# Fused four-layer encoder step: an early activation, weight parts split on two engines, the sample's tiles stacked for the transposes

## The chip, the core and the metric

The kernel runs on one core of a Trainium2 chip. The metric is device time in microseconds (us) for one execution. Five engines work side by side, each through its own instruction list in order: TensorE (PE, matrix products and transposes), VectorE (DVE), ScalarE (ACT), GpSimd (POOL) and SyncE (SP), which here issues every transfer (DMA). An instruction that waits holds back all that stands behind it on its own engine.

## The reference, cut to what matters

One inference step through four layers A, B, C, A. The input is 512 prompt tokens and 64 sample tokens, 1024 wide; the sample tokens attend to cached keys and values as well.

```python
for i in range(DEPTH):                      # kinds A, B, C, A
    z = rmsnorm(x, norm_g) @ w_in           # q, k, v and a gate in one projection
    q, k = rmsnorm(q, q_g), rmsnorm(k, k_g) # per head (C: low-rank q, latent kv, rotary part)
    o = attend(q, concat(cache, k), concat(cache, v), scale, bias, mask)
    x = x + (o * silu(gate)) @ w_out
return x_prompt, x_sample, new_a_k, new_a_v, new_b_k, new_b_v, new_c_kv, new_c_kr   # prompt and sample
```

A attends over a band of nine 64-token chunks with a relative bias, B over a window of 128 with four key heads and sinks, C over all the past through a 256-wide latent. The new keys and values and the rolled caches are outputs too.

## The kernel before

**Arithmetic.** Everything is 32-bit. Each operand of a product is split into a rounded high part and the rest, so one product is three matrix instructions. `load_w` (L132) loads a 128x512 weight piece (tile `ws`, L140 or L137), ACT writes its high part `wh` (L129) and the engine in `weng[0]` subtracts to get the low part `wl` (L130). That engine is POOL for the first eight pieces (`weng[0] = G` ahead of the opening loop) and DVE or POOL later. `wh` and `wl` have eight buffers each, `ws` four.

**Tiling.** The 576 tokens are four tiles of 128 and one of 64, the sample's. `mm_tok` (L161) is one tile's projection: three matrix instructions per piece for 128 tokens (L172 to L174). For the sample, its high and low parts are 128 columns of one operand, so there are two instructions (L177, L178), and the two halves of the result are added through the tile `hl` (ACT L182, DVE L183), which has one buffer.

**A unit** of work is one tile of one projection: `mm_tok`, a norm (`rstd`: DVE L124, POOL L125), a scaling into a tile of 128 x 512 (`qs`, three buffers; for the sample `half0` or `half1`, whose lower 64 rows stay zero), four or two PE transposes (`tr`, L187), and copies of the result out of PSUM.

**The opening.** For each of eight row blocks of the input, `x` and one weight piece are loaded, `feed` scales the block into `T` (ACT L199, DVE L200, ACT L202), squares it (ACT L204 for the first block, L207 then) and adds the squares (`acc`, DVE L208). `stats` then sums `acc` over partitions on PE (L213), from which the norms' factors `rr` come (DVE L215, POOL L217).

**Layer B** writes the newest keys to an output: for the last prompt tile and the sample tile DVE scales the transposed keys into a staging tile `st` (L529), and a DMA takes it to `bkT` (L530). `st`, like the cached keys' staging tile `kst`, is a buffer of the tag `hl`. **Layer C** loads the cached latent into a staging tile `cst`, also of tag `hl` (L790), issues six copies of caches from DRAM to DRAM behind it (`copy_caches`, L473 to L476), and splits `cst` into the high and low parts of the latent `lat` (ACT L129, POOL L130). POOL also makes the pow of each norm (L125) and the rotary parts of the queries (`qs`, L727 to L731). PE then transposes the queries and multiplies the latent with the key and value weights `kvb`.

**What sets the order.** Nothing is ordered by hand but the units of a stage. A scheduler with a timeline of its own decides when each instruction is put on its engine's list, so a small change can reorder lists far away from it. Buffers are rings: a tile with n buffers waits for the user n tiles ago.

Of the kernel before, what the change touches and what calls it, by code (L numbers as in the profile page):

```python
# [13 lines left out]
AF = mybir.ActivationFunctionType  # L14
# [14 lines left out]
QSB = 3  # L29
# [11 lines left out]
def encoder_step(ctx: ExitStack, tc: tile.TileContext, I, O):  # L41
# [12 lines left out]
    def sb(n, tag, bufs=None, dt=F32, pool=work):  # L54
        return pool.tile([128, n], dt, tag=tag, name=tag, bufs=bufs)
# [51 lines left out]
    ep = sb(5, "ep", pool=const)  # L107

# [77 lines left out]
    def tr(out, in_, perm=None):  # L186
        PE.transpose(out, in_, perm or ident)  # L187

# [116 lines left out]
    def layer_a(li, xT, first=None):  # L305
        w = I["a_w_in"][li]
        with tc.tile_pool(name=f"la{li}", bufs=1, reuse_waits="tile") as lp:
# [20 lines left out]
            def qk_units(pr):  # L328
                st = []

                def unit(t, t0, tn):
# [11 lines left out]
                    qs = rows_of(tn)  # L343
                    V.tensor_tensor(out=v3(qs[:tn], 128), in0=v3(p, 128), in1=bc(r.unsqueeze(2), tn, 4, 128), op=ALU.mult)
                    pt = v3(ps_t(), 128)
                    for j in range(4):
                        perm = ident if j > 1 else flip if tn == 128 else flip2
                        tr(pt[:, j, :], qs[:, j * 128 : j * 128 + 128], perm)
# [129 lines left out]
    def layer_b(xT):  # L478
        w = I["b_w_in"][0]
        with tc.tile_pool(name="lb", bufs=1, reuse_waits="tile") as lp:  # L480
# [14 lines left out]
            kst = v3(sb(512, "hl", 1), 128)  # L495
# [10 lines left out]
            for t, (t0, tn) in enumerate(TT):  # L506
# [18 lines left out]
                if t > 2:  # L525
                    o0 = t0 - 384
                    ld(O["bv"][o0 : o0 + tn], vt[:tn, t, :])
                    st = v3(sb(512, "hl", 1), 128)[:64, :, :tn]
# [5 lines left out]
            def q_units(g):  # L534
                w_ = []

                def unit(t, t0, tn):
# [10 lines left out]
                    qs = rows_of(tn)[:, :256]  # L548
                    V.tensor_tensor(out=v3(qs[:tn], 64), in0=v3(p, 64), in1=bc(r.unsqueeze(2), tn, 4, 64), op=ALU.mult)
                    pt = v3(ps_t()[:, :256], 128)  # L550
                    for j in range(2):
                        tr(pt[:, j, :], qs[:, j * 128 : j * 128 + 128])
# [138 lines left out]
    def layer_c(xT):  # L691
        w = I["c_w_in"][0]
        with tc.tile_pool(name="lc", bufs=1, reuse_waits="tile") as lp:
# [52 lines left out]
            for t, (t0, tn) in enumerate(TT):  # L746
# [5 lines left out]
                c = rows_of(tn)  # L752
                V.scalar_tensor_tensor(out=c[:tn], in0=p, scalar=r, in1=qag[:tn], op0=ALU.mult, op1=ALU.mult)
                pt = v3(ps_t(), 128)
                for j in range(4):
                    tr(pt[:, j, :], c[:, j * 128 : j * 128 + 128])
# [32 lines left out]
            cst = v3(sb(512, "hl", 1), 256)  # L789
# [167 lines left out]
    with tc.tile_pool(name="xp0", bufs=1) as xp:  # L957
        load_gain(0)
        for k in range(KD):
            xk = sb(TOK, f"x{k}", pool=xp)  # L960
            ld(xk, I["xT"][128 * k : 128 * k + 128, :])
            first.append(load_w([I["a_w_in"][0][128 * k : 128 * k + 128, 2048:2560]], 512))
            if k == 0:
                acc = new_acc(xp)
            feed(k, xk, gains[0], xT, xp, V, acc)
        ld(ident, I["ident"])
# [151 lines left out]
```

## Time and profile before

| | |
|---|---|
| median of three runs | 1255.45 us (1251.99 to 1255.57) |
| the profiled execution | 1254.89 us, of which the span of the trace is 1252.8 us |
| PE busy | 1225.8 us (98%) |
| DVE, ACT, POOL busy | 756.6 us (60%), 658.5 us (53%), 361.1 us (29%) |
| DMA | 125.11 MB, mean 100 GB/s |

The profile gives times from the start of the span. A row of a timeline is the start, the length, the engine, the line, the operation, the tile written and the tiles read, and in brackets how long the engine stood idle ahead of it and what ended that. PEclk is the clock granted to TensorE as a share of full speed. The rows of the changed kernel have other line numbers, 1 to 18 higher.

### The profile page before, as it was taken

Reading aid. Unit: us, or ns where it says so; the run is one execution under the profiler, and the core shown is the slowest. Engines: PE = TensorE matmul, PEld = TensorE weight load, DVE = VectorE, ACT = ScalarE, POOL = GpSimd, SP = SyncE. Lnnn points to the kernel's source line nnn. Section 1 sums busy time; section 2 is a strip of 40 time slices with the busy share of each in tenths; the row PEclk is TensorE's granted clock in tenths of the full one; section 3 lists DMA queues with packets and bytes.
Section 4 is the critical chain, followed back from the end, with each engine's and each line's share of the span. In section 5 each row is a group of like instructions: output and inputs, shape, how many; then the busy total and the mean of one; then the engine's idle time right before and its main releaser. Section 6 shows DMA issues by size and latency. Waiting matters only on the chain.

```text
span 1252.8 us, 22331 instructions
## 1 busy us (share of the span) xinstructions
PE 1225.8 (98%) x8015; PEld 1095.7 (87%) x8015; DVE 756.6 (60%) x2055; ACT 658.5 (53%) x1653; POOL 361.1 (29%) x425
## 2 busy tenths in 40 slices
PE   6999999999999999999999999999999999999998
PEld 5888898999989899899998887876998888889998
DVE  6266544755468888754577767676633665347552
ACT  5345543654436776643466767676533454436430
POOL 6422202222222120232285544440320322012130
PEclk9999999999999999999999999999999999999999
DMA  6333341434422231342272101112343233314331
GB/s 211 118 95 90 121 129 52 150 119 139 141 78 71 58 92 56 119 142 93 60 247 57 51 22 44 35 51 73 124 152 117 87 99 103 131 58 134 101 130 48
DMA packets 106046, 125.11 MB, mean 100 GB/s; under 512 B 11856, under 2 KB 83952, under 8 KB 105872
## 3 DMA queue, kind: packets, MB, share of 16 engines
q1 hardware_dynamic: 105936, 123.69, 31.7%
q8 instruction: 63, 1.03, 0.4%
q14 instruction: 47, 0.39, 0.1%
HBM read 103.73 MB, written 24.26 MB: 102 GB/s over the span
## 4 chain that ended last, share of the span: by engine, by line
PE 92%; DVE 3%; ACT 2%; issue 1%; DMA 1%; POOL 1%; SPq 0%; DVEq 0%; ACTq 0%
PE mm L174 11%; PE mm L173 11%; PE mm L172 11%; PE t L187 8%; PE mm L249 5%; PE mm L250 5%; PE mm L251 5%; PE mm L294 3%; PE mm L295 3%; PE mm L293 3%; PE o L412 3%; PE s L890 3%; PE mm L177 2%; PE mm L178 2%; PE o L900 2%; PE s L295 2%
## 5 line engine op out<-in xcount | busy, mean ns | idle before, releaser
L125 POOL TENSOR_TENSOR nv<-nv,mhalf 128x4 f32<-128x4 f32 (+6 forms) x127 | 139.8, 1108 | 350.1 <-DVE nv L124 306.7
L172 PE MATMUL mm<-wh,T 128*128 128x512 f32 (+2 forms) x600 | 217.5, 372 | 9.8 <-ACT wh L129 7.5
L173 PE MATMUL mm<-wl,T 128*128 128x512 f32 (+2 forms) x600 | 219.8, 369 | 0.0
L174 PE MATMUL mm<-wh,T 128*128 128x512 f32 (+2 forms) x600 | 219.5, 369 | 0.0
L130 DVE TENSOR_TENSOR wl<-ws,wh 128x512 fp32r<-128x512 f32 (+2 forms) x272 | 185.3, 696 | 47.4 <-ACT wh L129 43.3
L129 ACT ACTIVATE wh<-ws 128x512 fp32r<-128x512 f32 (+2 forms) x288 | 169.9, 615 | 65.8 <-PE mm L294 27.3
L249 PE MATMUL mm<-T,wh 128*128 128x288 f32 x512 | 155.7, 304 | 0.1
L250 PE MATMUL mm<-T,wh 128*128 128x288 f32 x512 | 153.5, 300 | 0.0
L251 PE MATMUL mm<-T,wl 128*128 128x288 f32 x512 | 153.3, 300 | 0.0
L172 PEld LDWEIGHTS mm<-wh,T 128*128 128x128 f32 x600 | 114.2, 191 | 26.4 <-ACT wh L129 7.5
L174 PEld LDWEIGHTS mm<-wh,T 128*128 128x128 f32 x600 | 114.6, 191 | 16.7 <-issue 0.2
L173 PEld LDWEIGHTS mm<-wl,T 128*128 128x128 f32 x600 | 114.9, 192 | 16.1 <-issue 0.5
L249 PEld LDWEIGHTS mm<-T,wh 128*128 128x128 f32 x512 | 96.2, 188 | 3.1 <-issue 1.9
L250 PEld LDWEIGHTS mm<-T,wh 128*128 128x128 f32 x512 | 96.3, 188 | 1.8 <-issue 1.7
L259 POOL TENSOR_TENSOR o<-o,sq 128x288 f32<-128x288 f32 x52 | 45.4, 874 | 179.7 <-DVE sq L257 91.3
L251 PEld LDWEIGHTS mm<-T,wl 128*128 128x128 f32 x512 | 96.1, 188 | 1.0 <-issue 1.0
L294 PE MATMUL mm<-oT,wh 128*128 128x288 f32 x320 | 94.7, 297 | 0.5 <-DVE oT L279 0.5
L293 PE MATMUL mm<-oT,wh 128*128 128x288 f32 x320 | 93.3, 297 | 1.9 <-ACT oT L278 1.9
L295 PE MATMUL mm<-oT,wl 128*128 128x288 f32 x320 | 94.0, 296 | 0.0
L382 DVE CUSTOM_DVE_ANT_0 ex<-s,bias 128x128 f32<-128x128 f32 (+1 forms) x64 | 30.4, 484 | 57.8 <-PE s L404 46.7
L293 PEld LDWEIGHTS mm<-oT,wh 128*128 128x128 f32 x320 | 59.9, 189 | 2.3 <-ACT oT L278 2.3
L294 PEld LDWEIGHTS mm<-oT,wh 128*128 128x128 f32 x320 | 60.4, 189 | 1.5 <-DVE oT L279 1.5
(289 smaller groups left out, 2886.4 us busy)
## 6 DMA issues: line engine op xcount, KB each, us to landing
ws<-in_a_w_in SPq DMA_DIRECT2D x64, 256.0 KB, 3.0
ws<-in_a_w_in SPq DMA_DIRECT2D x128, 128.0 KB, 2.3
ws<-in_b_w_in SPq DMA_DIRECT2D x40, 256.0 KB, 3.2
ws<-in_a_w_out SPq DMA_DIRECT2D x32, 256.0 KB, 3.1
xd<-x SPq DMA_DIRECT2D x24, 288.0 KB, 3.0
x<-xd SPq DMA_DIRECT2D x24, 288.0 KB, 5.9
ws<-in_c_w_in SPq DMA_DIRECT2D x24, 256.0 KB, 3.2
x<-in_xT SPq DMA_DIRECT2D x16, 288.0 KB, 6.3
```

The costliest lines, as they stand in the source:

```text
L125: G.tensor_tensor(out=r, in0=r, in1=bc(mhalf[:tn], tn, n), op=ALU.pow)
L129: S.activation(h, src, AF.Copy)
L130: (eng or G).tensor_tensor(out=l, in0=src, in1=h.bitcast(F32), op=ALU.subtract)
L172: PE.matmul(out, xh, h[:, ws], start=(i == 0), stop=False)
L173: PE.matmul(out, xh, l[:, ws], start=False, stop=False)
L174: PE.matmul(out, xl, h[:, ws], start=False, stop=(i == last))
L249: PE.matmul(p, wh, xT[:, k, cs], start=(k == 0), stop=False)
L250: PE.matmul(p, wh, xT[:, k, ls], start=False, stop=False)
L251: PE.matmul(p, wl, xT[:, k, cs], start=False, stop=(k == KD - 1))
L293: PE.matmul(p, wh, oT[:, k, cs], start=(k == 0), stop=False)
L294: PE.matmul(p, wh, oT[:, k, ls], start=False, stop=False)
L295: PE.matmul(p, wl, oT[:, k, cs], start=False, stop=(k == KD - 1))
```

## The change

1. At the very beginning ACT squares one column of a constant into one column of `rr`, which is written again later.
2. In the opening loop `weng[0]` alternates: DVE makes `wl` of the pieces 0, 2, 4 and 6, POOL of 1, 3, 5 and 7. Behind the loop it is POOL again.
3. `pairs_of` is new. Units of a 128-token tile are as before. For the sample, two 64-row blocks go one under the other into a full `qs` tile, by two DVE operations of half the width, and one transpose takes both: two in place of four in layers A and C, one in place of two in layer B. `half0` and `half1` stay in use elsewhere.
4. `kst` and `st` in layer B take a buffer of the tag `ex` (four of them), and `cst` in layer C one of `sq` (two), in place of `hl`.

PE's list is 22 transposes shorter.

```diff
@@ -105,6 +105,7 @@
     rb = sb(TOK, "rb", pool=const)
     rr = sb(5, "rr", pool=const)
     ep = sb(5, "ep", pool=const)
+    S.activation(rr[:, 0:1], mhalf, AF.Square)
 
     late = [None]
     weng = [V]
@@ -185,6 +186,16 @@
 
     def tr(out, in_, perm=None):
         PE.transpose(out, in_, perm or ident)
+
+    def pairs_of(tn, n, w, op):
+        qs = rows_of(tn) if tn == 128 else sb(512, "qs", QSB)
+        pt = v3(ps_t()[:, : n * tn], tn)
+        if tn == 128:
+            op(v3(qs[:, : n * w], w), slice(0, n))
+        else:
+            for e in range(2):
+                op(v3(qs[64 * e : 64 * e + 64, : n * w // 2], w), slice(e, n, 2))
+        return qs, pt, 128 // tn
 
     def hl_evac(dst_h, dst_l, src):
         S.activation(dst_h, src, AF.Copy)
@@ -340,12 +351,13 @@
                     ss = sb(4, "nss", pool=tiny)[:tn]
                     V.tensor_reduce(out=ss, in_=v3(sq, 128), axis=AX, op=ALU.add)
                     r = rstd(ss, tn, 4, 1.0 / 128, t)
-                    qs = rows_of(tn)
-                    V.tensor_tensor(out=v3(qs[:tn], 128), in0=v3(p, 128), in1=bc(r.unsqueeze(2), tn, 4, 128), op=ALU.mult)
-                    pt = v3(ps_t(), 128)
-                    for j in range(4):
-                        perm = ident if j > 1 else flip if tn == 128 else flip2
-                        tr(pt[:, j, :], qs[:, j * 128 : j * 128 + 128], perm)
+                    def put(out, js):
+                        V.tensor_tensor(out=out, in0=v3(p, 128)[:, js], in1=bc(r[:, js].unsqueeze(2), tn, out.shape[1], 128), op=ALU.mult)
+
+                    qs, pt, n = pairs_of(tn, 4, 128, put)
+                    for i in range(4 // n):
+                        perm = ident if i * n > 1 else flip if tn == 128 else flip2
+                        tr(pt[:, i * n : i * n + n, :], qs[:, i * 128 : i * 128 + 128], perm)
                     cs = slice(t0, t0 + tn)
                     V.tensor_scalar(out=kf[:, :, cs], in0=pt[:, 2:4, :tn], scalar1=kg, scalar2=None, op0=ALU.mult)
                     if t in (0, 4):
@@ -492,7 +504,7 @@
             vc = sb(256, "vc", pool=lp)
             ld(vc, I["cache_b_v"][0, 0].rearrange("t h d -> t (h d)"))
 
-            kst = v3(sb(512, "hl", 1), 128)
+            kst = v3(sb(512, "ex", 4), 128)
             with tc.issue_after(late[0]):
                 for e in range(2):
                     ld(kst[64 * e : 64 * e + 64], I["cache_bkT"].rearrange("h p t -> p h t"))
@@ -525,7 +537,7 @@
                 if t > 2:
                     o0 = t0 - 384
                     ld(O["bv"][o0 : o0 + tn], vt[:tn, t, :])
-                    st = v3(sb(512, "hl", 1), 128)[:64, :, :tn]
+                    st = v3(sb(512, "ex", 4), 128)[:64, :, :tn]
                     V.tensor_scalar(out=st, in0=pt[:64, :, :tn], scalar1=kg[:64], scalar2=None, op0=ALU.mult)
                     ld(O["bkT"].rearrange("h p t -> p h t")[:, :, o0 : o0 + tn], st)
 
@@ -545,11 +557,15 @@
                     ss = sb(4, "nss", pool=tiny)[:tn]
                     V.tensor_reduce(out=ss, in_=v3(sq, 64), axis=AX, op=ALU.add)
                     r = rstd(ss, tn, 4, 1.0 / 64, t)
-                    qs = rows_of(tn)[:, :256]
-                    V.tensor_tensor(out=v3(qs[:tn], 64), in0=v3(p, 64), in1=bc(r.unsqueeze(2), tn, 4, 64), op=ALU.mult)
-                    pt = v3(ps_t()[:, :256], 128)
-                    for j in range(2):
-                        tr(pt[:, j, :], qs[:, j * 128 : j * 128 + 128])
+                    def put(out, js):
+                        i0, n = (js.start, 2) if js.step else (0, 4)
+                        src, f = (p, r) if n == 4 else (p[:, 128 * i0 : 128 * i0 + 128], r[:, 2 * i0 : 2 * i0 + 2])
+                        V.tensor_tensor(out=out.rearrange("p a (b c) -> p (a b) c", c=64), in0=v3(src, 64),
+                                        in1=bc(f.unsqueeze(2), tn, n, 64), op=ALU.mult)
+
+                    qs, pt, n = pairs_of(tn, 2, 128, put)
+                    for i in range(2 // n):
+                        tr(pt[:, i * n : i * n + n, :], qs[:, i * 128 : i * 128 + 128])
                     for e in range(2):
                         a, b = slice(64 * e, 64 * e + 64), slice(64 - 64 * e, 128 - 64 * e)
                         dst = q[:, e, :, t0 : t0 + tn] if t < 4 else qm[:, :, e, :]
@@ -749,11 +765,13 @@
                 junk = sb(512, "sq", 2)[:tn]
                 S.activation(junk, p, AF.Square, accum_out=ss)
                 r = rstd(ss, tn, 1, 1.0 / 512, t)
-                c = rows_of(tn)
-                V.scalar_tensor_tensor(out=c[:tn], in0=p, scalar=r, in1=qag[:tn], op0=ALU.mult, op1=ALU.mult)
-                pt = v3(ps_t(), 128)
-                for j in range(4):
-                    tr(pt[:, j, :], c[:, j * 128 : j * 128 + 128])
+
+                def put(out, js):
+                    V.scalar_tensor_tensor(out=out, in0=v3(p, 128)[:, js], scalar=r, in1=v3(qag, 128)[:tn, js], op0=ALU.mult, op1=ALU.mult)
+
+                c, pt, n = pairs_of(tn, 4, 128, put)
+                for i in range(4 // n):
+                    tr(pt[:, i * n : i * n + n, :], c[:, i * 128 : i * 128 + 128])
                 l0 = lo_at(t0, TOK)
                 hl_evac(cq[:, :, t0 : t0 + tn], cq[:, :, l0 : l0 + tn], pt[:, :, :tn])
 
@@ -786,7 +804,7 @@
                 S.activation(ckv[:, :, k0 : k0 + tn], pt[:, 0:2, :tn], AF.Copy)
                 V.tensor_tensor(out=ckv[:, :, l0 : l0 + tn], in0=pt[:, 0:2, :tn],
                                 in1=ckv[:, :, k0 : k0 + tn].bitcast(F32), op=ALU.subtract)
-            cst = v3(sb(512, "hl", 1), 256)
+            cst = v3(sb(512, "sq", 2)[:, :512], 256)
             copy_caches(ld(cst, I["cache_ckvT"].rearrange("(k p) t -> p k t", p=128)))
             l0 = lo_at(SEQ, NK)
             split(ckv[:, :, 512:768], ckv[:, :, l0 : l0 + PAST], cst)
@@ -959,10 +977,12 @@
         for k in range(KD):
             xk = sb(TOK, f"x{k}", pool=xp)
             ld(xk, I["xT"][128 * k : 128 * k + 128, :])
+            weng[0] = (V, G)[k % 2]
             first.append(load_w([I["a_w_in"][0][128 * k : 128 * k + 128, 2048:2560]], 512))
             if k == 0:
                 acc = new_acc(xp)
             feed(k, xk, gains[0], xT, xp, V, acc)
+        weng[0] = G
         ld(ident, I["ident"])
         end = stats(xp, acc)
         ld(flip, I["flip"])
```

**DVE in the opening.** Before (`T` are the low parts of the blocks, `acc` the sums of squares):

```order
L200 SCALAR_TENSOR_TENSOR T_98<-x0_103,ga0_94,T_98 128x576
L200 SCALAR_TENSOR_TENSOR T_98<-x1_117,ga0_94,T_98 128x576
L208 TENSOR_TENSOR acc_111<-acc_111,xsq_128 128x576
L200 SCALAR_TENSOR_TENSOR T_98<-x2_131,ga0_94,T_98 128x576
L208 TENSOR_TENSOR acc_111<-acc_111,xsq_142 128x576
L200 SCALAR_TENSOR_TENSOR T_98<-x3_145,ga0_94,T_98 128x576
L208 TENSOR_TENSOR acc_111<-acc_111,xsq_156 128x576
L200 SCALAR_TENSOR_TENSOR T_98<-x4_159,ga0_94,T_98 128x576
L208 TENSOR_TENSOR acc_111<-acc_111,xsq_170 128x576
```

After:

```order
L211 SCALAR_TENSOR_TENSOR T_99<-x0_104,ga0_95,T_99 128x576
L131 TENSOR_TENSOR wl_109<-ws_106,wh_108 128x512
L211 SCALAR_TENSOR_TENSOR T_99<-x1_118,ga0_95,T_99 128x576
L219 TENSOR_TENSOR acc_112<-acc_112,xsq_129 128x576
L211 SCALAR_TENSOR_TENSOR T_99<-x2_132,ga0_95,T_99 128x576
L219 TENSOR_TENSOR acc_112<-acc_112,xsq_143 128x576
L131 TENSOR_TENSOR wl_137<-ws_134,wh_136 128x512
L211 SCALAR_TENSOR_TENSOR T_99<-x3_146,ga0_95,T_99 128x576
L219 TENSOR_TENSOR acc_112<-acc_112,xsq_157 128x576
L211 SCALAR_TENSOR_TENSOR T_99<-x4_160,ga0_95,T_99 128x576
L219 TENSOR_TENSOR acc_112<-acc_112,xsq_171 128x576
```

Two of the four `wl` that DVE has taken over (L131) stand among these rows; the other two follow behind the next blocks. On PE, 67 matrix instructions stand ahead of `stats` in both orders.

**PE in layer C,** where the queries are transposed. Before (`mm_7953` are keys and values from the latent `lat` and the weights `kvb`, `t` the transposed queries):

```order
L173 MATMUL mm_7953<-wl_7944,lat_7046 128x256
L174 MATMUL mm_7953<-wh_7943,lat_7046 128x256
L172 MATMUL mm_7953<-wh_7949,lat_7046 128x256
L173 MATMUL mm_7953<-wl_7950,lat_7046 128x256
L174 MATMUL mm_7953<-wh_7949,lat_7046 128x256
L187 MATMUL t_7698<-ident_76,qs_7679 96x128 x4
L187 MATMUL t_7737<-ident_76,qs_7718 96x128 x4
L187 MATMUL t_7776<-ident_76,qs_7757 96x128 x4
```

After (`mm_7917` is the gate's sum that stood ahead of `mm_7953`, now `mm_7958`; `t_7703` to `t_7781` are the queries):

```order
L261 MATMUL mm_7917<-T_6517,wh_7808 128x288
L262 MATMUL mm_7917<-T_6517,wl_7809 128x288
L188 MATMUL t_7703<-ident_76,qs_7684 96x128 x4
L188 MATMUL t_7742<-ident_76,qs_7723 96x128 x4
L188 MATMUL t_7781<-ident_76,qs_7762 96x128 x4
L173 MATMUL mm_7958<-wh_7948,lat_7051 128x256
L173 MATMUL mm_7987<-wh_7948,lat_7051 128x256
```

The twelve keys-and-values instructions that stood ahead of the three groups of transposes now stand behind them.

**POOL in layer C,** a little earlier. Before (`lat` is the latent's low part, `nv` the pows of three query tiles, `krz` and `qs` rotary parts):

```order
L731 TENSOR_TENSOR krz_7053<-r1_7589,r2_7590 64x32
L125 TENSOR_TENSOR nv_7686<-nv_7686,mhalf_81 128x8
L125 TENSOR_TENSOR nv_7725<-nv_7725,mhalf_81 128x8
L125 TENSOR_TENSOR nv_7764<-nv_7764,mhalf_81 128x8
L130 TENSOR_TENSOR lat_7046<-hl_7604,lat_7046 128x2x256
L817 TENSOR_TENSOR qs_7679<-qs_7679,nv_7686 128x4x32
```

After:

```order
L131 TENSOR_TENSOR lat_7051<-sq_7609,lat_7051 128x2x256
L747 TENSOR_TENSOR krz_7058<-r1_7594,r2_7595 64x32
L126 TENSOR_TENSOR nv_7691<-nv_7691,mhalf_81 128x8
L126 TENSOR_TENSOR nv_7730<-nv_7730,mhalf_81 128x8
L126 TENSOR_TENSOR nv_7769<-nv_7769,mhalf_81 128x8
L835 TENSOR_TENSOR qs_7684<-qs_7684,nv_7691 128x4x32
```

The split of the latent stood behind the three pows and now stands ahead of them. On SP the load of the latent and the six cache copies moved ahead of the loads of the two `kvb` pieces.

**PE at the end of layer B.** Before (`o_6145` are the prompt heads, `o_6215` the sample's attention, `mm_6460` the output projection):

```order
L627 MATMUL o_6145<-pb_6143,v_3668 64x256 x2
L627 MATMUL o_6145<-pb_6136,v_3668 64x256 x2
L627 MATMUL o_6145<-pb_6066,v_3668 64x256 x2
L627 MATMUL o_6145<-pb_6059,v_3668 64x256 x2
L666 MATMUL o_6215<-pts_6213,vc_3670 64x128 x2
L669 MATMUL o_6215<-pts_6213,v_3668 64x128 x2
L293 MATMUL mm_6460<-oT_6257,wh_6438 128x288
```

After (the same tiles are `o_6150` and `o_6220`):

```order
L261 MATMUL mm_6393<-T_3156,wh_6283 128x288
L262 MATMUL mm_6393<-T_3156,wl_6284 128x288
L260 MATMUL mm_6393<-T_3156,wh_6283 128x288
L261 MATMUL mm_6393<-T_3156,wh_6283 128x288
L262 MATMUL mm_6393<-T_3156,wl_6284 128x288
L260 MATMUL mm_6393<-T_3156,wh_6289 128x288
L261 MATMUL mm_6393<-T_3156,wh_6289 128x288
L262 MATMUL mm_6393<-T_3156,wl_6290 128x288
L260 MATMUL mm_6393<-T_3156,wh_6289 128x288
L261 MATMUL mm_6393<-T_3156,wh_6289 128x288
L262 MATMUL mm_6393<-T_3156,wl_6290 128x288
L682 MATMUL o_6220<-pts_6218,vc_3671 64x128 x2
```

Eleven gate instructions (L260 to L262) moved in between the prompt heads' products and the sample's.

## Rows read from the trace of the kernel before

**Rows 1.** The page: engines' busy time, the chain, one group of instructions.

```profile
PE 1225.8 (98%) x8015; PEld 1095.7 (87%) x8015; DVE 756.6 (60%) x2055; ACT 658.5 (53%) x1653; POOL 361.1 (29%) x425
...
PE 92%; DVE 3%; ACT 2%; issue 1%; DMA 1%; POOL 1%; SPq 0%; DVEq 0%; ACTq 0%
...
L130 DVE TENSOR_TENSOR wl<-ws,wh 128x512 fp32r<-128x512 f32 (+2 forms) x272 | 185.3, 696 | 47.4 <-ACT wh L129 43.3
```

**Rows 2.** Waits of PE: line, releaser: us in total, times, longest.

```profile
PE mm L172 <- DVE hl L183: 2.6, 2, 2.3
...
PE mm L293 <- ACT oT L278: 1.9, 2, 1.0
...
PE o L666 <- ACT o L303: 0.8, 1, 0.8
```

**Rows 3.** Timelines of ACT, PE, DVE and POOL in the opening.

```profile
4.25 1.28 ACT L199 ACT_TABLE_LOAD   x1 [4.25 <-DMA x<-in_xT]
...
7.47 1.65 PE L172 MATMUL mm<-wh,T 128*128 128x512 f32 x3 [7.47 <-ACT wh L129]
...
27.05 1.47 PE L213 MATMUL t<-ones,acc 128*128 128x2 f32 x10 [2.48 <-DVE acc L208]
...
9.32 0.75 DVE L208 TENSOR_TENSOR acc<-acc,xsq 128x576 f32<-128x576 f32 x1
...
11.75 1.85 DVE L208 TENSOR_TENSOR acc<-acc,xsq 128x576 f32<-128x576 f32 x1
...
23.41 3.58 DVE L208 TENSOR_TENSOR acc<-acc,xsq 128x576 f32<-128x576 f32 x2
...
7.49 1.28 POOL L130 TENSOR_TENSOR wl<-ws,wh 128x512 fp32r<-128x512 f32 x1 [5.20 <-ACT wh L129]
...
17.51 5.36 POOL L130 TENSOR_TENSOR wl<-ws,wh 128x512 fp32r<-128x512 f32 x3 [2.75 <-ACT wh L129]
```

**Rows 4.** Windows: busy us (instructions) of each engine, PEclk, DMA share, GB/s.

```profile
27.00:31.00 4.00, 3.95 (x16) 3.46 (x17) 0.66 (x7) 0.04 (x1) 2.21 (x3) 0.62 0.74 200
...
369.00:372.00 3.00, 3.00 (x17) 3.00 (x16) 2.42 (x9) 1.20 (x4) 2.06 (x3) 0.55 0.13 33
...
526.00:529.00 3.00, 1.23 (x13) 0.87 (x12) 1.00 (x3) 2.07 (x7) 1.59 (x2) 1.00 0.94 272
529.00:533.00 4.00, 3.99 (x19) 3.76 (x18) 3.99 (x4) 3.59 (x8) 3.80 (x3) 0.59 0.96 331
...
644.00:648.00 4.00, 2.79 (x20) 2.29 (x21) 0.15 (x1) 2.14 (x6) 3.56 (x10) 1.00 0.64 203
```

**Rows 5.** Timelines of DVE, ACT and PE in layer B, 361 to 372.

```profile
363.80 0.73 DVE L529 TENSOR_SCALAR hl<-t,par 64x512 f32<-64x512 f32 x1
...
367.38 0.59 ACT L182 ACTIVATE hl<-mm 64x512 f32<-64x512 f32 x1 [1.62 <-DMA out_bkT<-hl]
...
368.84 0.36 PE L172 MATMUL mm<-wh,T 128*128 128x256 f32 x1 [2.29 <-DVE hl L183]
```

**Rows 6.** Timeline of PE, layer B: four sample transposes and the next.

```profile
373.28 0.60 PE L187 MATMUL t<-ident,half 128*128 128x128 f32 x4
373.71 0.38 PE L187 MATMUL t<-ident,qs 128*128 128x128 f32 x2
```

**Rows 7.** Timelines of PE, POOL and ACT in layer C, 630 to 652.

```profile
644.21 0.39 PE L172 MATMUL mm<-wh,lat 128*128 128x256 f32 x1 [0.27 <-DVE hl L183]
...
645.75 1.27 PE L187 MATMUL t<-ident,qs 128*96 128x128 f32 x8
648.00 0.64 PE L187 MATMUL t<-ident,qs 128*96 128x128 f32 x4 [0.98 <-POOL qs L731]
...
634.28 4.95 POOL L125 TENSOR_TENSOR nv<-nv,mhalf 128x8 f32<-128x8 f32 x3
...
647.49 0.45 POOL L731 TENSOR_TENSOR qs<-r,r 128x128 f32<-128x128 f32 x1
...
636.18 0.63 ACT L129 ACTIVATE lat<-hl 128x512 fp32r<-128x512 f32 x1 [2.00 <-DMA hl<-in_cache_ckvT]
```

## The prediction

> **What bounds the kernel now.** I read the page first: PE is busy 98% of the span and makes up 92% of the chain that ended last [rows 1]. So time is won in three ways only: PE gets fewer instructions, it waits less, or it runs less at half clock. Then I read the list of PE's waits [rows 2]: they are few and short, so each has a place of its own. I went to those places that the change touches, in timelines of the engines there [rows 3, 5, 7], and last to windows that show the granted clock beside the busy time [rows 4], because a wait of PE can be paid twice.
>
> The second payment is in [rows 4]. After the wait of 2.48 us at 27.05 [rows 3] the window from 27 to 31 has a granted clock of 0.62 with PE fully busy; after the wait of 2.29 at 368.84 [rows 5] it is 0.55; after a stretch of 3.00 us with PE busy for 1.23 it is 0.59. That is a mix of the two levels, 2.4 and 1.2 GHz. The last of these windows gives the price: (1 − 0.59) × 4.00 = 1.6 us of work not done. A window with 1.21 us of idle PE in 4.00 (644 to 648) kept 1.00. So a short wait costs itself, and one over 2 us costs itself and 1.6 more.
>
> **The change part by part.**
>
> *The opening, start.* ACT's table load takes 1.28 us and starts only when the first block of x has landed, at 4.25 [rows 3]. PE's first matrix instruction waits on ACT's first `wh`, at 7.47. With the one-column activation ahead, which waits on no transfer, the load runs before 4.25, ACT's chain starts 1.28 earlier, and so does PE: 7.47 − 1.28 = 6.2. The added activation costs nothing as long as the transfer covers it. PE then runs the same 67 instructions up to the sums of `stats` without a wait, in both orders; it came there at 27.05 − 2.48 = 24.57 and now comes at 23.3.
>
> *The opening, end.* There PE waits for the last `acc` on DVE, which ends at 23.41 + 3.58 = 26.99 [rows 3]. DVE and POOL hinder each other: the same `acc` addition takes 0.75 alone and 1.85 beside a POOL subtraction, 1.10 more; POOL's takes 1.28 alone and 5.36 / 3 = 1.79 when they alternate. So the two engines' work adds up rather than overlaps. The Trainium skill has the reason (SBUF — State Buffer, Who interferes with whom): an operation of VectorE with two SBUF inputs and one of GpSimd that reads SBUF hold a shared port in turn, each for its whole length. That speaks against splitting the low parts over two engines; if the two ran side by side, the last `acc` would be done before PE arrives and the gain would be 0.7 larger than I take below. By the rows, four subtractions leave POOL, 4 × 1.28 = 5.1, and four come to DVE, at 0.70 each [rows 1], 2.8. The sum shrinks by 2.3. The earlier start is worth between 0.4 and 1.28 here, because the transfers of later blocks do not come earlier. The last `acc` ends between 26.99 − 3.6 = 23.4 and 24.3. I take 24.0 for PE's start, near the later end, since every x has to land at its old time: a gain of 27.05 − 24.0 = 3.05, and a wait of 0.7 in place of 2.48. Bounds: 1.28 (the wait stays as long) and 3.75 (none is left). A wait of 0.7 is nearer to the window that kept its clock than to the three that lost it, so 1.6 more are saved. Together 4.65.
>
> *Layer B, the wait for `hl`.* DVE writes the staging tile at 363.80 and a DMA reads it; only when that has landed may ACT write the one buffer again for the sample tile, at 367.38; DVE adds the halves, and PE waits 2.29 for it at 368.84 [rows 5]. With `st` in another ring the sample's halves are added as soon as PE has made them. The wait of 2.3 goes, with the half clock behind it: 3.9. What is late next is DVE, busy 2.42 of the 3.00 us from 369 to 372 [rows 4]. Bounds: 0 (DVE gives it all back) and 3.9. I take the upper, because with the wait gone DVE has the idle time of that stretch ahead as well.
>
> *Layer B, end.* PE waits 0.8 for the prompt heads' copies (L303) and then, in one of the two waits on `oT`, 1.0 [rows 2]. Eleven gate instructions now stand in the first of these; they are PE work that was there anyway, so 0.8 is saved. The second wait stays, its cover is gone with them. Whether the half clock of 529 to 533 [rows 4] goes too is open: 0 to 1.6. I take 0, because PE still does only eight short products between two waits.
>
> *Transposes.* 22 go. Four take 0.43 from start to the next start [rows 6], 0.108 each: 2.4. All but two stand among other PE work in layers A and B. The 13 added DVE operations, of half the width, lie beside that: DVE is at 60% of the span [rows 1]. Bounds: 0 (each falls into a wait) and 2.4.
>
> *Layer C.* Before, PE spent 644.21 to 645.75, that is 1.5 us, on twelve keys-and-values instructions while POOL made the rotary parts, and waited 0.98 for the last of these, which ended at 647.49 + 0.45 = 647.94 [rows 7]. Now the transposes come first, and PE stands from about 643.8 until the same 647.94, with only the transposes to do: the twelve instructions come behind and cost 1.5. Idle time is then over 2 of some 4 us, nearer to the window of 526 to 529 than to that of 644 to 648 [rows 4], so I count 1.6 for the clock. The loss is 3.1; its bounds are 0 (POOL is done sooner) and 5.6 (below, E).
>
> *The rest* of layers A, B and C is put in another order here and there with no wait on either side that the trace shows; I take 0, with 1.5 either way.
>
> **Sum.** 4.65 + 3.9 + 0.8 + 2.4 − 3.1 = 8.65. Against the profiled execution, 1254.89 (a span of 1252.8 and 2.1 around it), that is 1246.2; against the median of 1255.45, which is 0.56 higher, **1246.8**. The median is what will be compared, so this is the forecast.
>
> **The rivals.**
>
> A. *The clock does not follow the length of the wait.* For: between the long waits and the window that stayed at 1.00 the trace has few cases. Then half clock stays in the opening, or comes anew elsewhere: one to two times 1.6, so 1248.4 to 1250.0. The Trainium skill (TensorE: Matmul & The Clock Gate, What's actually happening) says that the window in which activity is judged runs freely and isn't set by the kernel's start; by that, where a wait falls decides with its length. No row here shows that phase.
>
> B. *The opening keeps its wait.* If the transfers and not the sum of DVE and POOL set the last `acc`, everything moves by the 1.28 of the start alone, the wait stays near 2.5 and the clock drops: 1246.8 + 4.65 − 1.28 = 1250.2. Against it: the last rows of DVE stand packed with POOL's [rows 3].
>
> C. *DVE takes the place of `hl`.* In layer B DVE is the next engine, and 3.9 come back as waits on it a little later: 1250.7.
>
> D. *It does little of what it says:* two of B, C and "the transposes fall into waits" at once. B and C give 1246.8 + 3.4 + 3.9 = 1254.1, B and the transposes 1246.8 + 3.4 + 2.4 = 1252.6.
>
> E. *Slower.* In layer C POOL's split of the latent now stands ahead of the three pows, which started at 634.28 before [rows 7]. POOL takes its list in order, so if the cached latent lands late, the pows, the rotary parts and PE's transposes wait for it, one for one. ACT had the latent at 636.18 and took 0.63 over it [rows 7]; at that time POOL would stand for 636.8 − 634.3 = 2.5 us: 1249.3. Slower than before it gets when the landing is 8.65 later than POOL's arrival, about 642.3 on the old scale, 6 us after the old landing; slower by over 0.3% from about 646. For it: six cache copies and the weights share the transfers there. Against it: the load now stands ahead of the copies, and needs no buffer of `hl`.
>
> **Chances.** Forecast 0.45, with a range of its own from 1243 to 1250; A 0.12; B 0.15; C 0.10; D 0.10; E 0.08. 0.3% is 3.8 us, about what a measurement of this kernel can tell from no change: under 1251.7 is faster, over 1259.2 slower. Faster is most of the forecast, A and B, and two thirds of C: 0.79. Same is D and the tails of B, C and E: 0.16. Slower is half of E and a little of the unseen: 0.05. The low end, 1242.5, has the clock kept in layer C (1.6) and at the end of layer B (1.6), and a little for no wait in the opening; the high end, 1253.5, reaches into D.
>
> **What would show it.** PE's first instruction at 6.2, `stats` on PE at 24.0 after a wait under 1, and a clock of 1.00 from 24 to 28. No wait on `hl` in layer B, and no window under 1.00 there. The sample's attention at the end of layer B without a wait in front. Around the queries' transposes in layer C, waits of PE on POOL's `qs` of together 3 us. 22 transposes fewer. Wrong would be: a wait of over 2 us on `acc`, a new wait on DVE in layer B over 2 us, or POOL standing for the latent.

## The result, and the profile after

The changed kernel takes 1245.16 us (median of four runs, 1244.52 to 1248.99) where the kernel before took 1255.18; the ratio is 0.9929, 95% interval 0.9917 to 0.9941, so 7.4 to 10.4 us less. 1246.8 was forecast. Two later series of the same kernel gave 0.9930 (0.9916 to 0.9944) and 0.9912 (0.9897 to 0.9926).

The page of the changed kernel: span, busy time of each engine.

```profile
span 1243.5 us, 22309 instructions
...
PE 1220.9 (98%) x7993; PEld 1090.6 (88%) x7993; DVE 757.0 (61%) x2072; ACT 659.6 (53%) x1654; POOL 353.4 (28%) x421
```

The share of PE is as before [rows 1]: it has 22 instructions fewer, and the span is 9.3 us shorter. The waits of PE (line, releaser: us in total, times, longest), to be read against [rows 2]:

```profile
PE t L188 <- POOL qs L747: 2.0, 2, 1.0
PE mm L304 <- ACT oT L289: 1.9, 2, 1.0
...
PE mm L174 <- DVE wl L131: 0.9, 1, 0.9
...
PE t L224 <- DVE acc L219: 0.2, 1, 0.2
```

The wait on `hl` is gone and so are the 0.8 ahead of the sample's attention at the end of layer B; the wait on ACT's `oT` is what it was. On POOL's `qs` in layer C there are two waits where there was one of 0.98 [rows 7]. In the opening the 2.48 on `acc` [rows 3] have become 0.17, with 0.93 on a low part ahead of it. Timelines of ACT, PE, DVE and POOL in the opening:

```profile
0.72 1.28 ACT L108 ACT_TABLE_LOAD   x1 [0.72 <-PEq L1107]
...
6.20 1.65 PE L173 MATMUL mm<-wh,T 128*128 128x512 f32 x3 [6.20 <-ACT wh L130]
...
24.21 0.51 PE L174 MATMUL mm<-wl,T 128*128 128x512 f32 x1 [0.93 <-DVE wl L131]
24.88 1.28 PE L224 MATMUL t<-ones,acc 128*128 128x2 f32 x10 [0.17 <-DVE acc L219]
...
22.38 1.77 DVE L131 TENSOR_TENSOR wl<-ws,wh 128x512 fp32r<-128x512 f32 x1
24.08 0.75 DVE L219 TENSOR_TENSOR acc<-acc,xsq 128x576 f32<-128x576 f32 x1
...
20.37 3.23 POOL L131 TENSOR_TENSOR wl<-ws,wh 128x512 fp32r<-128x512 f32 x2 [0.29 <-ACT wh L130]
```

The table load now runs at 0.72, PE starts at 6.20, and the sums are on PE at 24.88, 2.17 earlier than before. The instruction ahead of the sums needs the seventh low part, which DVE makes at 22.38 in 1.77 us instead of 0.70, beside POOL's last two (20.37). Windows (busy us and instructions of PE, PEld, DVE, ACT, POOL, then PEclk, DMA share, GB/s):

```profile
27.00:31.00 4.00, 4.00 (x12) 3.12 (x11) 1.07 (x5) 1.15 (x2) 1.49 (x2) 0.57 0.59 160
...
358.00:364.00 6.00, 6.00 (x52) 6.00 (x52) 5.73 (x11) 4.52 (x10) 0.17 (x1) 1.00 0.78 218
364.00:368.00 4.00, 4.00 (x36) 4.00 (x35) 2.91 (x10) 1.23 (x4) 3.04 (x4) 1.00 0.55 154
...
518.00:521.00 3.00, 2.05 (x19) 1.65 (x18) 1.68 (x4) 2.68 (x8) 1.42 (x2) 1.00 0.87 259
521.00:525.00 4.00, 3.55 (x25) 3.32 (x26) 3.96 (x4) 4.00 (x9) 3.86 (x3) 1.00 1.01 348
634.00:638.00 4.00, 3.02 (x24) 2.67 (x23) 1.20 (x4) 1.64 (x5) 3.69 (x10) 1.00 0.68 193
```

The half clock after the opening is still there (0.57), though the wait is 1.1 and not 2.5. The work of 369 and 529, where [rows 4] had 0.55 and 0.59, now lies at about 362 and 521, and there nothing is below 1.00. The end of layer B, on PE:

```profile
519.39 0.44 PE L682 MATMUL o<-pts,vc 128*64 128x128 f32 x4
...
521.06 0.53 PE L304 MATMUL mm<-oT,wh 128*128 128x288 f32 x2 [1.01 <-ACT oT L289]
...
522.24 0.40 PE L305 MATMUL mm<-oT,wh 128*128 128x288 f32 x1 [0.39 <-DVE oT L290]
```

The eleven gate products stand ahead of 519.39, which has no wait in brackets now; the 1.01 on `oT` stay, and 0.39 on DVE's part of `oT` have come behind them. Layer C, PE and POOL:

```profile
628.23 1.10 PE L237 MATMUL t<-ex,ones 128*128 128x512 f32 x2 [0.67 <-DVE lat L805]
...
636.21 0.64 PE L188 MATMUL t<-ident,qs 128*96 128x128 f32 x4
637.84 0.64 PE L188 MATMUL t<-ident,qs 128*96 128x128 f32 x4 [0.98 <-POOL qs L747]
639.46 0.64 PE L188 MATMUL t<-ident,qs 128*96 128x128 f32 x4 [0.98 <-POOL qs L747]
...
626.38 1.28 POOL L131 TENSOR_TENSOR lat<-sq,lat 128x512 fp32r<-128x512 f32 x1
...
638.95 0.45 POOL L747 TENSOR_TENSOR qs<-r,r 128x128 f32<-128x128 f32 x1
```

PE waits 0.67 for the latent at 628.23, reaches the transposes at 636.21 just as the first rotary part is done, and waits 0.98 twice; the last part ends at 638.95 + 0.45 = 639.40.

**Where the time went.** The same PE instruction can be looked up in both traces. The table gives its start in a trace minus that in the kernel before, as the median over a 20 us stretch that begins at the time named (on the scale of before); a step from one column to the next is what was won or lost between them. Stretches at half clock are part of it. a1, r1 and so on are the kernels of the next section; u2 and u2b are one kernel.

| trace | 40 | 320 | 380 | 560 | 720 | 920 | 1220 |
|---|---|---|---|---|---|---|---|
| changed | −2.17 | −2.96 | −7.09 | −8.56 | −8.40 | −8.55 | −9.35 |
| r1, the same again | −4.63 | −5.45 | −9.57 | −11.04 | −10.79 | −9.68 | −10.45 |
| r2, the same again | −4.69 | −5.51 | −8.50 | −9.98 | −8.16 | −7.09 | −7.88 |
| a1 | −1.30 | −1.28 | −2.09 | −3.54 | −2.99 | −3.11 | −3.06 |
| a2 | −3.42 | −3.44 | −2.75 | −2.74 | −2.88 | −3.00 | −3.00 |
| a3 | −4.43 | −4.45 | −4.41 | −5.85 | −5.70 | −5.64 | −5.64 |
| a4 | −0.04 | −0.02 | −3.94 | −4.16 | −3.63 | −3.08 | −3.04 |
| u1 | −4.38 | −5.22 | −9.35 | −10.82 | −9.72 | −8.62 | −9.38 |
| u2 | −5.26 | −6.05 | −10.18 | −11.64 | −11.41 | −11.52 | −12.35 |
| u2b | −4.55 | −5.36 | −8.44 | −9.92 | −9.70 | −9.89 | −10.72 |
| u3 | −5.68 | −5.66 | −8.77 | −9.01 | −8.84 | −9.00 | −8.98 |
| v1 | −4.36 | −5.01 | −7.80 | −9.27 | −8.77 | −8.96 | −9.75 |
| v2 | −5.48 | −6.29 | −10.42 | −11.89 | −11.49 | −11.68 | −12.47 |

### The profile page after: what moved, and what is told of

It is laid out like the page before. It is cut to its first block, busy times and chain, and to the rows that moved or that the text cites. A ratio compares the mean times of both kernels' runs of the same rounds, so it can differ in the third digit from the quotient of the medians.

```text
span 1243.5 us, 22309 instructions
## 1 busy us (share of the span) xinstructions
PE 1220.9 (98%) x7993; PEld 1090.6 (88%) x7993; DVE 757.0 (61%) x2072; ACT 659.6 (53%) x1654; POOL 353.4 (28%) x421
## 4 chain that ended last, share of the span: by engine, by line
PE 92%; DVE 4%; DMA 1%; ACT 1%; issue 1%; POOL 0%; SPq 0%; DVEq 0%; ACTq 0%
PE mm L175 11%; PE mm L174 11%; PE mm L173 11%; PE t L188 8%; PE mm L260 5%; PE mm L261 5%; PE mm L262 5%; PE mm L305 3%; PE mm L306 3%; PE mm L304 3%; PE o L424 3%; PE mm L178 3%; PE mm L179 3%; PE s L908 3%; PE o L918 2%; PE s L306 2%
## 5 line engine op out<-in xcount | busy, mean ns | idle before, releaser
L131 DVE TENSOR_TENSOR wl<-ws,wh 128x512 fp32r<-128x512 f32 (+2 forms) x276 | 189.1, 700 | 46.1 <-ACT wh L130 41.9
L260 PE MATMUL mm<-T,wh 128*128 128x288 f32 x512 | 156.0, 305 | 0.0
L262 PE MATMUL mm<-T,wl 128*128 128x288 f32 x512 | 153.4, 300 | 0.0
L260 PEld LDWEIGHTS mm<-T,wh 128*128 128x128 f32 x512 | 96.3, 188 | 3.2 <-issue 2.2
L262 PEld LDWEIGHTS mm<-T,wl 128*128 128x128 f32 x512 | 96.1, 188 | 1.0 <-issue 1.0
L350 ACT ACTIVATE sq<-mm 128x512 f32<-128x512 f32 x32 | 19.1, 598 | 80.2 <-PE mm L175 80.0
L305 PEld LDWEIGHTS mm<-oT,wh 128*128 128x128 f32 x320 | 60.0, 188 | 1.8 <-DVE oT L290 1.8
```

The source lines that it names most:

```text
L131: (eng or G).tensor_tensor(out=l, in0=src, in1=h.bitcast(F32), op=ALU.subtract)
L260: PE.matmul(p, wh, xT[:, k, cs], start=(k == 0), stop=False)
L262: PE.matmul(p, wl, xT[:, k, cs], start=False, stop=(k == KD - 1))
L305: PE.matmul(p, wh, oT[:, k, ls], start=False, stop=False)
```

## The experiments

**Theory:** each part acts at its own place: the start of the opening, the added-up work of DVE and POOL at its end, the one buffer `hl` in layer B, PE's transposes; and a wait of PE is paid again by half clock only where it is long. **Rivals:** half clock does not follow the length of a wait (A); the early start makes the opening's gain alone; DVE takes the place of `hl` (C); what layer C loses or wins is given back.

**Each part alone: a1_act, a2_wl, a3_open, a4_stage.** The kernel before with one or two edits of the change.

```diff
 a1 and a3:
+    S.activation(rr[:, 0:1], mhalf, AF.Square)
 a2 and a3, in the opening loop, and behind it:
+            weng[0] = (V, G)[k % 2]
+        weng[0] = G
 a4:
-            kst = v3(sb(512, "hl", 1), 128)
+            kst = v3(sb(512, "ex", 4), 128)
-                    st = v3(sb(512, "hl", 1), 128)[:64, :, :tn]
+                    st = v3(sb(512, "ex", 4), 128)[:64, :, :tn]
```

> The kernel before with part 1 alone, the one-column activation. Theory (the opening ends when DVE and POOL have done their added-up work, and every x lands at its old time): PE starts at 6.2 in place of 7.47, the last sum of squares moves by 0.4 to 1.3 us only, PE waits 2.5 to 3.4 us for it and the half-clock window stays; time 0.4 to 1.3 us less. Rival (the early start makes the whole gain of the opening): 2.2 us less.

Measured: 1252.63 us, ratio 0.9986 (0.9973 to 0.9998). PE starts at 6.20, the sums come at 25.76, and the window behind stays at half clock: 1.30 in the opening, at the theory's upper end, with a wait of 1.83 that is shorter than expected. The rest of what the trace gained, 0.8 at 380 and 1.45 at 560, stands at places that the edit does not touch: the half clock of 369 and 529 did not come in this execution, although PE waited longer for `hl` than before, 2.61 in place of 2.29:

```profile
PE mm L173 <- DVE hl L184: 3.4, 2, 2.6
```

The times alone, 0.3 to 3.4 us less, do not tell the theory from the rival; the trace does.

> The kernel before with part 2 alone, the low parts on two engines in turn. Theory: four subtractions of 1.28 leave the added-up work and four of 0.70 come, so the last sum of squares comes 1.5 to 2.3 us earlier; PE starts at 7.47 as before; time 1.5 to 2.3 us less, or 3 to 4 if the half-clock window goes as well. Rival (the transfers set the end): under 0.5 us less.

Measured: 1251.68, ratio 0.9978 (0.9967 to 0.9989). PE and windows:

```profile
25.26 1.28 PE L213 MATMUL t<-ones,acc 128*128 128x2 f32 x10 [0.17 <-DVE acc L208]
...
27.00:31.00 4.00, 4.00 (x19) 3.33 (x18) 1.30 (x10) 1.27 (x2) 1.86 (x3) 1.00 0.80 208
364.00:370.00 6.00, 3.91 (x20) 3.94 (x21) 3.50 (x10) 2.07 (x5) 2.80 (x3) 0.72 0.26 77
```

PE starts at 7.51, the sums come 1.79 earlier, with 0.17 of wait, and this time the clock stays at 1.00: 3.42 in the opening, as the theory has it for that case. The wait on `hl` is there, 2.99 here, with half clock (0.72 in the second window).

> The kernel before with parts 1 and 2 together, nothing else of the change. Theory: the opening as in the changed kernel, the sums on PE at 24.9, 2.2 us less, one half-clock window at about 27; the rest as before. Rival (the early part moves work of the layers behind it): more or less than 2.2 by over 0.5 us.

Measured: 1251.02, ratio 0.9966 (0.9954 to 0.9979). The sums at 24.23, 2.82 earlier, and no half clock behind: 4.43 in the opening. The expected half clock did not come, in the same opening in which it came in the changed kernel. But the wait is not the same: 0.17 ahead of the sums and none on the low part, against 1.10 together there. So this run does not tell rival A from the theory.

> The kernel before with part 4's layer B half alone: the two staging tiles of layer B in the ring of four. Theory (the wait on the one buffer is what PE loses at 366): the wait of 2.3 us on the sample's sum goes, with the half clock behind it where it came; 2.4 less, or 4.0 where the window goes too; the rest as before. Rival (VectorE is late next in layer B): 2 us or more of new waits on VectorE up to 425, under 1 us gained.

Measured: 1251.47, ratio 0.9982 (0.9972 to 0.9991). From 320 to 380 the trace gains 3.92, the wait with its window, as in the theory. Of the waits of PE

```profile
PE t L213 <- DVE acc L208: 2.3, 1, 2.3
PE mm L293 <- ACT oT L278: 2.2, 3, 1.0
PE s L594 <- DVE nm L600: 2.1, 2, 1.2
```

the one on `hl` is gone; `s` on `nm` is 2.1 where the profile of before has 1.5. That is what VectorE takes back: 0.6, not 2, and 0.5 on its `pb`, which before has at 423, is gone in exchange. The half clock of 529 did not come, and the shift in finer steps is −5.76 at 533; but PE then stands for `oT` (L293 has 2.2 in three waits, before 1.9 in two [rows 2], and L294 waits 0.13 and 0.33 around 531), and at 543 it is −4.17 again. These waits are 0.8 of the 1.6 lost there; the rest isn't resolved.

**The same kernel again: r1_after, r2_after.** No edit.

> The changed kernel once more, for more runs. Theory (each half-clock window costs about 1.6 us and comes in some executions and not in others, at the same waits): the times spread over several us in steps near 1.6, as those of the kernel before do; median 9 to 11 us below the kernel before; the waits in the trace as in the first, the windows at other places or in another number. Rival (the windows belong to the code): the same window at about 27 and no other.

Measured: 1245.95 (1242.48 to 1247.55), ratio 0.9930, 8.9 below the kernel before. In its trace, PE, DVE, POOL and windows:

```profile
24.16 1.17 PE L224 MATMUL t<-ones,acc 128*128 128x2 f32 x10
...
20.06 0.74 DVE L219 TENSOR_TENSOR acc<-acc,xsq 128x576 f32<-128x576 f32 x1
...
18.30 6.15 POOL L131 TENSOR_TENSOR wl<-ws,wh 128x512 fp32r<-128x512 f32 x3 [4.17 <-DMA ws<-in_a_w_in]
...
27.00:31.00 4.00, 4.00 (x20) 3.30 (x19) 1.08 (x5) 1.96 (x3) 0.74 (x2) 1.00 0.57 139
861.00:866.00 5.00, 4.73 (x17) 2.35 (x19) 1.12 (x5) 2.15 (x5) 0.00 (x0) 0.66 0.58 211
```

No wait ahead of the sums, no half clock behind them; half clock at 862 instead, where the changed kernel's first trace has none. And the last `acc` ends at 20.06 + 0.74 = 20.80, not at 24.83: here DVE runs each operation from 14.66 on in its own time. POOL's three subtractions take 6.15, but not evenly: the first 3.66, over DVE's last three operations, the other two 1.28 and 1.29.

> The changed kernel a third time, beside the three below. Theory (whether a wait is followed by half clock differs from execution to execution): none to two half-clock windows, at places with the waits of the first two traces; sums of the opening on PE between 24.1 and 24.9. Rival: a window at the place of one of the two earlier traces again.

Measured: 1244.81 (1242.46 to 1246.69), ratio 0.9912. In its trace:

```profile
364.55 0.66 PE L188 MATMUL t<-ident,half 128*128 128x128 f32 x4 [0.64 <-DVE half L528]
...
27.00:31.00 4.00, 4.00 (x19) 3.30 (x19) 1.07 (x5) 1.96 (x3) 0.81 (x2) 1.00 0.78 172
639.00:643.00 4.00, 4.00 (x21) 3.94 (x20) 3.58 (x10) 2.69 (x7) 4.00 (x3) 0.57 0.43 115
```

Half clock now after the waits on `qs` in layer C, and once more at 864, none after the opening. With it comes 0.64 of wait on DVE's `half` in layer B, which the other two traces do not have. So rival A holds: the two waits of 0.98 in layer C, the same in all three traces, are followed by half clock in r2 alone, and the two of 0.70 and 0.84 at 860 in r1 and r2 but not in the first trace. Each half clock costs 1.1 to 1.7.

**All eight low parts on DVE: u2_allv, u2b_allv** (the second is the same kernel again).

```diff
-            weng[0] = (V, G)[k % 2]
+            weng[0] = V
```

> The changed kernel with all eight low parts of the opening on DVE, none on POOL. Theory (the wait that is left in the changed kernel, 0.93 us for a low part and 0.17 for the sums, comes from DVE and POOL holding each other up): 21 DVE operations of 0.68 to 0.82 follow each other without the 1.1 extra, PE reaches the sums without a wait, 1.1 us less than the changed kernel, and the half-clock window at 27 goes with the wait, 1.6 more: 2.7 less, about 12.3 less than the kernel before. First rival (the window comes from the ten tiny products of the sums or from its phase, not from the wait): 1.1 less than the changed kernel and the window stays. Second rival (DVE with eight more subtractions is the bound): no gain or a loss against the changed kernel.

> The changed kernel with all eight low parts of the opening on DVE, again, for more runs. Theory: the sums of squares are ready at about 21 and PE comes to the sums without a wait in every execution; 0 to 0.9 us less than the changed kernel, which waits in some executions only. Rival: no less than the changed kernel.

Measured: 1246.0, ratio 0.9926 (0.9908 to 0.9944), and 1245.65, ratio 0.9920 (0.9906 to 0.9934): no less than the changed kernel that these runs can tell. The traces, DVE and PE:

```profile
21.02 0.70 DVE L131 TENSOR_TENSOR wl<-ws,wh 128x512 fp32r<-128x512 f32 x1
...
24.20 1.17 PE L224 MATMUL t<-ones,acc 128*128 128x2 f32 x10
```

DVE is done at 21.72 and never slowed; PE comes to the sums without a wait, and the clock stays, in both. Against the first trace of the changed kernel that is 3.1 in the opening, against r1 0.6, and in the second series, with the sums at 24.91, nothing against r2. The theory is right on the wait. What it did not see is that the changed kernel waits only in some executions.

**One part undone: u1_cst, u3_pairs.**

```diff
 u1:
-            cst = v3(sb(512, "sq", 2)[:, :512], 256)
+            cst = v3(sb(512, "hl", 1), 256)
 u3, the whole body of pairs_of, for the sample too:
+        qs = rows_of(tn)
+        pt = v3(ps_t()[:, : n * 128], 128)
+        op(v3(qs[:tn, : n * w], w), slice(0, n))
+        return qs, pt, 1
```

> The changed kernel with the cached latent's staging tile of layer C in the one-buffer ring again. Theory (in the changed kernel the cache copies go ahead of the key and value weights, so their products can't stand between the queries' transposes): the products come before the second transposes again, one of the two waits on GpSimd's rotary parts goes, 0.5 to 1.3 us less than the changed kernel. Rival (the loss at 640 is given back by 700 anyway): within 0.3 us of it.

Measured: 1244.95, ratio 0.9923 (0.9911 to 0.9935): the same. In the trace layer C (560 to 720) loses 1.10, where the changed kernel loses 0.16 and r1 0.25. The products come before the second transposes, but PE waits

```profile
634.96 0.64 PE L188 MATMUL t<-ident,qs 128*96 128x128 f32 x4 [1.73 <-POOL qs L747]
...
638.25 0.64 PE L188 MATMUL t<-ident,qs 128*96 128x128 f32 x4 [0.77 <-POOL qs L747]
```

1.73 and 0.77, more than the two times 0.98. My theory of layer C fell. The rival did not come out in the trace either: nothing is given back here, the shift is −9.76 at 640 and −9.72 at 700, 0.9 more lost than in the changed kernel. The times of the two kernels do not show that difference.

> The changed kernel with part 3 undone: the sample's blocks transposed one at a time, 22 transposes more. Theory: 20 of them stand among other work of PE at 0.108 us, about 2.2 us more than the changed kernel, 0.8 of it in each layer A. Rival (they fall into waits): under 0.7 us more. In layer B the order moves as well: up to 1.5 either way.

Measured: 1247.22, ratio 0.9944 (0.9933 to 0.9956), 1.3 over r1 of the same series; the intervals overlap, so it is the trace that decides. From 40 to 320 it loses 0.02 where the changed kernel gains 0.79, and from 920 to 1220 it loses 0.02 against a gain of 0.80: 1.6 for the 16 transposes of the two layers A. From 380 to 560 it gains 0.24 against 1.47.

By the ratios the parts add up: 1.8 us for a1 and 2.8 for a2, 4.3 for both together (a3), 2.3 for a4 and 1.8 for the stacked transposes (u3 against r1). a3, a4 and the transposes make 8.3; the whole change is worth 8.8 to 11.0 in its three series. Each of these values is uncertain by 1 to 2 us.

**The latent's subtraction on DVE: v1_latv, and with u2's edit v2_best.**

```diff
-            split(ckv[:, :, 512:768], ckv[:, :, l0 : l0 + PAST], cst)
+            split(ckv[:, :, 512:768], ckv[:, :, l0 : l0 + PAST], cst, V)
```

> The changed kernel with the subtraction of the cached latent in layer C on DVE in place of GpSimd. Theory (GpSimd's chain of pows and rotary parts sets when the queries are transposed, and it is 1.28 us shorter without the subtraction): the last rotary part ends 1.0 to 1.3 us earlier against PE's other work, the two waits of 0.98 shrink by as much together, and 0.5 to 1.3 us are left at 700. Rival (what is lost at 640 is given back by 700 and so is what is gained): within 0.3 us of the changed kernel at 700.

Measured: 1244.82, ratio 0.9907 (0.9893 to 0.9922). Layer C loses 0.50, not less than the changed kernel. POOL, DVE and PE:

```profile
625.48 1.31 POOL L743 TENSOR_TENSOR r<-y,ex 64x32 f32<-64x32 f32 x1 [2.64 <-DVE y L790]
...
638.39 0.46 POOL L747 TENSOR_TENSOR qs<-r,r 128x128 f32<-128x128 f32 x1
...
626.00 0.68 DVE L131 TENSOR_TENSOR lat<-sq,lat 128x512 fp32r<-128x512 f32 x1
...
638.90 0.64 PE L188 MATMUL t<-ident,qs 128*96 128x128 f32 x4 [0.99 <-POOL qs L747]
```

The subtraction takes 0.68 on DVE at 626.00, and POOL's operation beside it 1.31 where it took 0.59 in the changed kernel. The last rotary part ends at 638.39 + 0.46 = 638.85; by the shift in the table that is 0.2 later than in the changed kernel, not 1.28 earlier. The rival is right: 0.25 to 0.34 more is lost by 720 than in r1 and the first trace, and nothing gained.

> Both of the last two edits on the changed kernel: the opening's low parts and the cached latent's on DVE. Theory: the two gains add, 0.5 to 2.2 us less than the changed kernel. Rival: within 0.3 us of it.

Measured: 1243.44 (1242.45 to 1245.07, four runs), ratio 0.9906 (0.9892 to 0.9921). It is the lowest median, but its interval lies on that of the changed kernel in the same series (0.9897 to 0.9926): the runs do not tell it from the changed kernel. Its trace has no half clock and a span 3.2 us shorter than the first of the changed kernel; the opening alone gives 3.3.

## Why the prediction was right, and where it was not

The time fell inside the range, 1.6 below the forecast. The mechanisms of the opening's start, of `hl` and of the transposes were right. But two terms were off by 2.5 to 3 us in opposite directions, the opening with its half clock and layer C, and cancelled in the execution that was compared; that the sum came so near is luck.

- **Start of the opening:** 1.28 forecast, 1.27 measured (7.47 to 6.20). Right.
- **End of the opening:** the sums on PE at 24.0 were forecast; 24.88, 24.16 and 23.98 came in the three traces of the same kernel. The last two are near 24.0 for another reason than mine: PE came there without a wait, but 0.9 and 0.7 later than the 23.3 forecast for it, because its first products ran at half clock up to 11.84 in r1 and 11.16 in r2 (10.91 before, with a start 1.27 later). The step on DVE, that its and POOL's times add up, holds in four of the seven traces with this opening (the last `acc` ends at 24.83, 23.92 in r2, 24.24 in v1, 24.17 in a3; 23.4 to 24.3 was forecast) and fails in three (20.80 in r1, 20.6 in u1 and u3), where DVE isn't held up from 14.7 on. The Trainium skill (SBUF — State Buffer, Who interferes with whom) has it: of two operations on the shared port it is the order of issue that decides which one blocks. The seven traces agree. In the four, POOL's third subtraction starts 0.15 to 0.24 ahead of DVE's scaling of the last block, and then the engines alternate, DVE at 1.77 to 1.85 an operation. In the three it starts 0.11 to 0.35 behind it and lasts 3.55 to 3.79, over DVE's last three operations. I used the prices of one order as if there were no other. I also did not see that PE's instruction ahead of the sums needs a low part that DVE makes between the last two `acc`: 0.93 of the wait moved there.
- **Half clock behind it:** 1.6 forecast, 0 in the compared trace, 1.6 to 1.7 in r1 and r2, which have no wait there. The step that failed is the rule at the top, that a short wait costs itself alone and one over 2 us costs 1.6 more. 1.1 of wait with ten tiny products behind was followed by half clock in the changed kernel, and 2.61 on `hl` in a1 was not, where 2.29 to 2.99 were in before, a2 and a3. The 0.76 and 1.01 of wait at the end of layer B are the same in before, a1 to a4 and u3, and half clock follows in before and a2 only. That is rival A.
- **Layer B, `hl`:** 3.9 forecast; 4.1 in the first two traces, and 3.92 with the edit alone. Right in mechanism, and in size against an execution that has the half clock of 369. In r2 it is 3.0, with DVE's `half` late by 0.64 there, and in u2b, u3 and v1 it is 2.8 to 3.1, with waits of 0.53, 0.42 and 0.84 at the same place: rival C, in part.
- **Layer B, end, and four transposes:** 0.8 + 0.43 = 1.2 forecast, and nothing for the half clock of 529. From 380 to 560 the trace gains 1.47, and 1.47 − 0.24 = 1.23 against u3, which has neither; but the steps are others. Up to 528 the shift goes from −7.09 to −7.49, so 0.40 of the 1.2 is there, though the wait of 0.76 is gone; what took the rest isn't resolved. The new wait on DVE's `oT` takes 0.38 (−7.11 at 529). Then the half clock that did not come gives 1.53 (−8.64 at 533), as it does in a1 (−2.10 to −3.62). In a4 and u3 it did not come either, and there PE lost 1.6 again by 543, with waits on `oT`. So the sum fits by luck, and the window that I counted at nothing made the gain.
- **Transposes in the layers A:** 16 × 0.108 = 1.7 forecast, 1.6 measured. Right.
- **Layer C:** a loss of 3.1 forecast, 0.16 to 0.25 measured, and 1.8 in r2; the waits on `qs` are 1.96 together and not 3. Two steps failed. The clock: 1.6 counted, which came in one of three traces. And the 1.5 of moved products: at the place itself PE's waits do rise, from 1.3 to 2.6 with the 0.67 on the latent, and the shift taken in finer steps loses 1.2 at 640 (−8.8 to −7.6), but 0.8 of it is back by 700 (−8.4). PE also did not stand at the transposes from 643.8 on: it came about 1 us later, for the wait of 0.67 on the latent ahead, just as the first rotary part was ready. I had priced the products at the place where they left, and not at the place where they went: behind the transposes, up to 700, PE's waits fall from 1.2 to 0.7. That the moved products fill them is argued; no run shows it, and it is not the whole 0.8.
- **E, the slower case:** POOL did not stand for the latent; its subtraction ran at 626.38, behind the rotary parts of the keys and without a wait.

What stays open: why half clock follows a given wait in one execution and not in the next, and why POOL's subtraction starts just ahead of DVE's scaling in one execution and just behind it in another. No run here holds either of them fixed.

## What to carry to other kernels

Price a stall at the end of a chain with what else its place can do: look for the next instruction on the waiting engine that needs something made between the links of that chain. Price work that is moved at the place to which it goes, not only where it left. And when terms hang on half clock or on two engines that slow each other, take several executions of one kernel before explaining a microsecond: the changed kernel took 1242.5 to 1249.0. In r2's series its three runs with a granted clock of 1.000 took 1242.46 to 1243.87, the three with 0.997 took 1245.75 to 1246.69.

## What the runs showed of the hardware

- PE's first products run at half spacing, 0.43 us for 128x512 in place of 0.227, for a time that differs between executions of the same opening. u3, then u1, PE:

```profile
8.93 0.63 PE L174 MATMUL mm<-wl,T 128*128 128x512 f32 x1
...
9.70 0.39 PE L174 MATMUL mm<-wl,T 128*128 128x512 f32 x1
...
11.46 0.63 PE L178 MATMUL s<-wh,T 128*128 128x512 f32 x1
...
12.32 0.88 PE L173 MATMUL mm<-wh,T 128*128 128x512 f32 x3
```

In u3 the spacing falls to 0.23 from 9.70 on, in u1 from about 12.3, with the same first product at 6.2. That is 7 products more at half clock and moved the sums from 23.10 to 24.40 with no wait at all. The clock records of these traces begin only at the rise (9.59 in u3, 12.33 in u1). Ahead of the first record a window reads 1.00, which is no measurement: there the spacing of the starts is what shows half clock.
- DVE's operations with two inputs and POOL's subtractions at the end of the opening go in one of two ways. Where POOL starts first they alternate, DVE at 1.77 to 1.85 and POOL at 1.39 to 1.81 each. Where DVE starts first it runs its next operations in 0.68 to 0.75 each, while one subtraction of POOL takes 3.55 to 3.79; POOL's next two take 1.27 to 1.29.
- ACT's first activation starts 0.02 after the table load ends (0.72 + 1.28 = 2.00, 2.02), so the load costs 1.28 here and no more.
